# Seven-product MLP: products chained in PSUM banks, two weight pairs side by side in up, sums moved off GpSimd, down's operands in up's places

## The chip, the cores and the metric

The kernel runs on one NeuronCore of a Trainium2 chip. Times are device microseconds of one execution. A matmul runs on TensorE (PE in the rows, PEld for its weight loads); VectorE is DVE, ScalarE is ACT, GpSimd is POOL, SyncE is SP. DMA transfers are issued by the queues of SP and ACT here and are carried out by 16 DMA engines.

## The reference

One decoder layer of 1024 tokens of width 1024: a mixer (windowed attention, a gated short convolution and attention into memory tokens, one output projection) and then the part that the change is about, the MLP:

```
h2 = rms_norm(x, g_pre_mlp)
f = square(relu(h2 @ w_up))            # 1024x1024 @ 1024x4096
f = f @ w_down                         # 1024x4096 @ 4096x1024
x = x + rms_norm(f, g_post_mlp)
```

All of it is float32.

## The kernel before, in words

**Precision.** Every large product is computed from pairs of fp32r tiles: a "hi" part, a rounded copy written by ACT (`copy`, L88), and a "lo" part, the remainder, subtracted by DVE (`lo_part`, L92). Three matmuls (hi hi, hi lo, lo hi) make one product; `mm3` (L100 to L103) is the helper for it. So each operand tile costs one ACT and one DVE instruction before PE can use it; `split` does both.

**Seven products.** Up and down are computed by a Strassen/Winograd scheme: both matrices are cut into quarters, and 7 products of sums of quarters take the place of 8. For up, the hidden activations h2 (transposed, quarters b11, b12, b21, b22) are the fixed operand: the sums t1 to t4 are formed and split once. The weights come in 16 **pairs** (`p`) of two blocks of 128 columns; for each pair the sums s1 to s4 of the quarters a11, a12, a21, a22 are formed, and product `(p, i)` takes the weight form and the h2 form that `FORMS[i]` names. Each product is 12 matmuls of 128x512 into one PSUM bank; up has 16 x 7 x 12 = 1344 of them (L1107 to L1109).

**Up, per product.** `prep` (L1082) loads the pair's raw weights (`w_raw`, L1034, an SP transfer of 512 KB into one of 5 stage buffers), lets POOL form the four sums of the pair (`s_sums`, L1075 to L1079), and splits the product's weight form into a free slot `wop`. `product` (L1101) issues the matmuls, `product_out` (L1112) empties the bank: product 1 and product 2 share one bank, 5 and 3 share another, and every other product has its own. The four quarters of each result are put together by DVE additions in SBUF tiles `ef`, squared-relu is ACT (Relu, Square) or one DVE instruction (`relu2`, L1099), then the sums s1 to s4 of the activations (L1151 to L1154) are formed on DVE, and all of it is stored to DRAM by `f_out` (L1096) **on ACT's queue**. PE's order is written by hand: `seq` lists the products, pair after pair, each product's operand prepared by `prep_next` two places ahead in the program. For the first seven products the order of ACT, DVE and POOL is written by hand too (`manual_schedule`); after that a scheduler of the framework orders those engines and SP from the program's dependences.

**Head of up.** The last row tile of the out-projection (`y_mm`, `y_post_*`, `h2_turn`) is finished while PE already works on products 1 and 2 of pairs 0 to 2, which need only b11 and b21. t1 to t3 (`t_sums`, L1017) need the last row tile, t4 is one POOL instruction of 128x2048 (`raw_t4`, L1244).

**Down.** After up its pools are closed (`up_pool.close()`) and new ones opened. Down has 2 chunks (halves of the contraction), 7 products each in the order 1, 2, 7, 6, 5, 4, 3 and 1, 7, 6, 5, 4, 2, 3, and 4 steps to a product; a step is 24 matmuls of 128x512 into 4 banks (`sub_mm`, L1312), so 56 steps and 1344 matmuls. `prep2` (L1300) makes a step's operands, two steps ahead: one 128x1024 tile of stored activations (`fraw`, loaded by `a_load`) and one of w_down (`r_b`, loaded by `b_load`, or a DVE sum of two of them), each split, into one of 6 slots `op`. Each product has its own accumulator `acc` of 4 tiles (7 of them). `evict` (L1344) copies the banks out in chunk 0 (ACT) and adds in chunk 1 (DVE, L1352); POOL combines the seven accumulators while chunk 1 runs (L1355 to L1367). `piece` and `finish` do the last norm, the residual sum and the store of each row tile.

Of the kernel before, what the change touches and what calls it, by code (L numbers as in the profile page):

```python
# [45 lines left out]
def hybrid_block(ctx, tc, x, mem, positions, g_pre_mix, g_mem, w_in, w_mem_kv, conv_w, g_attn_out,  # L46
                 g_conv_out, g_xattn_out, w_out, g_post_mix, g_pre_mlp, w_up, w_down, g_post_mlp,
                 ident_in, bias_in, invf_in, out):
    nc = tc.nc
# [918 lines left out]
    for n in ("b11", "b21", "b22"):  # L968
        TM[n] = [p2.tile([128, 4, 512], R, name=n + s, tag=n + s) for s in "hl"]
    raw_pool = ExitStack()  # L970
    pr = raw_pool.enter_context(pool("h2raw", 1, side="right"))
    RB = {n: pr.tile([128, 4, 512], F, name="raw_" + n, tag="raw_" + n) for n in ("b11", "b22", "b12", "b21")}
    yb_pool = ExitStack()
    yb = yb_pool.enter_context(pool("yb", 2, side="right"))
# [17 lines left out]
    def y_post_add(st, r):  # L992
        xr, ob = XR[st], OB[st]
        for h in range(2):
            cl = slice(h * 512, (h + 1) * 512)
            v.scalar_tensor_tensor(xr[:, cl], ob[:, cl], r, xr[:, cl], op0=OP.mult, op1=OP.add)
        nc.sync.dma_start(x1_d[st * 128:(st + 1) * 128], xr)
        s2 = small.tile([128, 1], F, name="s1b", tag="s1b")
        sumsq(s2, xr, 1024)
        return s2  # L1000
# [16 lines left out]
    def t_sums(i):  # L1017

        cl = slice(i * 128, i * 128 + 128)
        b11, b12, b22 = (RB[n][:, :, cl] for n in ("b11", "b12", "b22"))  # L1020
        v.tensor_sub(b11, b12, b11)
        v.tensor_sub(b12, b22, b12)
        v.tensor_sub(b22, b22, b11)

    T_OF = {"t1": "b11", "t2": "b22", "t3": "b12", "t4": "t4"}

    def t_split(n, c0, c1):
        split(TM[n][0][:, :, c0:c1], TM[n][1][:, :, c0:c1], RB[T_OF[n]][:, :, c0:c1])

# [14 lines left out]

    NPAIR = FF // 256
# [6 lines left out]
    SM, WO_, PB, EF = {}, {}, {}, {}  # L1052
    banks = [mm_bank, mm_bank, s_bank, s_bank, pt_bank, pt_bank, ot_bank, tp_bank]
    bn = [0]

    def next_bank():
        bn[0] += 1
        return banks[(bn[0] - 1) % 8]()
# [5 lines left out]
    def e_tile():  # L1064
        slot = e_free.pop(0)
        t = slot[0].tile([128, 512], F, name="ef", tag=slot[1]) if isinstance(slot[1], str) else slot[0][:, slot[1]]
        return slot, t
# [5 lines left out]
    def s_sums(p):  # L1073
        s1, s2, s3, s4 = (ps_.tile([128, 4, 128], F, name=f"s{i}", tag=f"s{i}") for i in range(1, 5))
        a11, a12, a21, a22 = (a_block(p, n) for n in ("a11", "a12", "a21", "a22"))  # L1075
        g.tensor_add(s1, a21, a22)
        g.tensor_sub(s2, s1, a11)
        g.tensor_sub(s3, a11, a21)
        g.tensor_sub(s4, a12, s2)  # L1079
        SM[p] = {"s1": s1, "s2": s2, "s3": s3, "s4": s4}  # L1080

    def prep(p, i):  # L1082

        n = FORMS[i][0]
        for ff in ([2 * p] if n in ("a11", "a12") else [2 * p, 2 * p + 1]):
            if ff not in WR:
                w_raw(ff)
        if n[0] == "s" and p not in SM:
            s_sums(p)
        slot, w = w_op()  # L1090
        split(w[:, 0], w[:, 1], SM[p][n] if n[0] == "s" else a_block(p, n))
        WO_[p, i] = slot, w

    def f_out(p, n, t):
        c, r = p // 8, p % 8 * 128
        nc.scalar.dma_start(f_d[c][n][r:r + 128], t)  # L1096

    def relu2(t):
        v.scalar_tensor_tensor(t, t, 0.0, t, op0=OP.max, op1=OP.mult)  # L1099

    def product(p, i):  # L1101
        th, tl = TM[FORMS[i][1]]
        slot, w = WO_.pop((p, i))
        prev = {2: 1, 3: 5}.get(i)
        b = PB[p, i] = PB[p, prev] if prev else next_bank()
# [6 lines left out]
    def product_out(p, i):  # L1112
        b = PB[p, i]
        e = EF.setdefault(p, {})
        if i == 1:
            e["u"] = e_tile()
            copy(e["u"][1], b)
        elif i == 2:
            t = (None, stage(512, name="ef")) if p < 3 else e_tile()
            nc.scalar.activation(t[1], b, AF.Relu)  # L1120
            nc.scalar.activation(t[1], t[1], AF.Square)
            f_out(p, "a11", t[1])
            if p > 2:
# [326 lines left out]
```

## Time and profile before

| what | value |
|---|---|
| time, median of 3 runs | 1220.71 us (1218.74 to 1222.88) |
| profiled execution, its own time | 1217.59 us |
| its span in the trace | 1215.8 us |
| PE busy | 1140.7 us, 94%, 5776 matmuls |
| DVE, ACT, POOL busy | 820.9, 579.7, 249.6 us |
| first matmul of up, last matmul of up | 535.85 us, 874.07 us |
| first matmul of down, last matmul of down | 882.88 us, 1206.29 us |

The span is what the trace covers; the profiled execution's own time has 1.8 us around it, and the median of the runs is 3.1 us above that execution. Everything up to about 535 us is the mixer. "Busy" adds up instructions, so 94% on PE does not say that only 6% can be won, nor where: that has to be read by stage.

### The profile page before, as it was taken

What the parts mean: (1) busy time and instruction counts of PE and PEld (TensorE: products, weight loads), DVE (VectorE), ACT (ScalarE), POOL (GpSimd) and SP (SyncE); (2) the same over time, 40 slices, a digit from 0 to 9 for tenths busy, and PEclk for the clock granted to TensorE, in tenths of its full rate; (3) what the DMA queues carried; (4) which work ended last, traced back from release to release, by engine and by line L of the source; (5) the groups of instructions that cost most, each with busy time, mean ns of one, the idle gap of its engine ahead of it and who ended that gap; (6) DMA issues with size and microseconds to landing.
All of it is one profiled execution on the core that took longest, in us unless ns stands there. A gap on an engine that the chain in (4) does not pass through costs nothing.

```text
span 1215.8 us, 15988 instructions
## 1 busy us (share of the span) xinstructions
PE 1140.7 (94%) x5776; PEld 966.1 (79%) x5776; DVE 820.9 (68%) x1380; ACT 579.7 (48%) x1096; POOL 249.6 (21%) x222
## 2 busy tenths in 40 slices
PE   6989999999999999986899999999789999999896
PEld 5879999897878778875778888888668888888684
DVE  6977676777677357657976666666466644697885
ACT  5675666657574445545333333333144454433342
POOL 2370201102020211104532222221000000025631
PEclk9989999999999999997999999999989999999898
DMA  7340100100212543333444444432493247332234
GB/s 228 122 118 6 48 23 18 38 8 9 67 31 62 164 166 139 121 112 96 147 156 149 150 153 155 156 130 104 159 368 122 98 162 263 135 103 90 85 132 180
DMA packets 119663, 145.05 MB, mean 119 GB/s; under 512 B 8736, under 2 KB 72864, under 8 KB 119584
## 3 DMA queue, kind: packets, MB, share of 16 engines
q1 hardware_dynamic: 103456, 114.67, 29.5%
q10 hardware_dynamic: 16128, 29.37, 6.5%
q8 instruction: 45, 0.74, 0.3%
q14 instruction: 34, 0.28, 0.1%
HBM read 102.06 MB, written 41.94 MB: 118 GB/s over the span
## 4 chain that ended last, share of the span: by engine, by line
PE 75%; DVE 10%; ACT 5%; DMA 4%; issue 3%; POOL 1%; SPq 1%; ACTq 0%; DVEq 0%; POOLq 0%
PE mm L101 7%; PE mm L102 7%; PE mm L103 7%; PE sc L103 3%; PE sc L101 3%; PE sc L102 3%; PE pt L103 2%; PE pt L102 2%; PE pt L472 2%; PE pt L101 2%; PE sc L1109 2%; PE mm L1107 2%; PE sc L1107 2%; PE sc L1108 2%; PE pt L1107 2%
## 5 line engine op out<-in xcount | busy, mean ns | idle before, releaser
L92 DVE TENSOR_TENSOR op<-fraw,op 128x1024 fp32r<-128x1024 f32 x56 | 71.5, 1280 | 88.0 <-ACT op L88 87.9
L88 ACT ACTIVATE op<-fraw 128x1024 fp32r<-128x1024 f32 x56 | 59.0, 1058 | 141.4 <-PE tp L103 65.2
L212 POOL TENSOR_TENSOR wl<-wraw,wh 128x384 fp32r<-128x384 f32 (+1 forms) x62 | 56.3, 936 | 293.1 <-ACT wh L88 291.4
L101 PE MATMUL mm<-wh,hh 128*128 128x384 f32 x256 | 91.5, 357 | 0.9 <-ACT wh L88 0.9
L102 PE MATMUL mm<-wl,hh 128*128 128x384 f32 x256 | 87.6, 342 | 0.3 <-DVE wl L212 0.2
L103 PE MATMUL mm<-wh,hl 128*128 128x384 f32 x256 | 87.6, 342 | 0.0
L92 DVE TENSOR_TENSOR op<-r_b,op 128x1024 fp32r<-128x1024 f32 x56 | 73.7, 1316 | 9.2 <-ACT op L88 9.2
L92 DVE TENSOR_TENSOR wop<-s,wop 128x512 fp32r<-128x512 f32 x64 | 49.3, 776 | 35.1 <-ACT wop L88 34.5
L88 ACT ACTIVATE wop<-wuraw 128x512 fp32r<-128x512 f32 x45 | 28.5, 633 | 91.2 <-DVE ef L1153 38.0
L92 DVE TENSOR_TENSOR tl<-pt,th 128x512 fp32r<-128x512 f32 (+1 forms) x96 | 60.0, 643 | 17.3 <-ACT th L88 16.5
L130 POOL TENSOR_TENSOR rstd<-ms,half_neg 128x1 f32<-128x1 f32 (+2 forms) x43 | 29.7, 692 | 193.8 <-DVE ms L127 177.3
L88 ACT ACTIVATE op<-r_b 128x1024 fp32r<-128x1024 f32 x56 | 58.6, 1046 | 12.8 <-PE sc L103 8.7
L461 ACT ACTIVATE P<-P,m 128x896 f32<-128x896 f32 (+3 forms) x64 | 49.7, 776 | 30.3 <-DVE m L459 29.6
L88 ACT ACTIVATE wop<-s 128x512 fp32r<-128x512 f32 x64 | 39.8, 628 | 49.7 <-PE pt L1109 9.4
L88 ACT ACTIVATE th<-pt 128x512 fp32r<-128x512 f32 (+1 forms) x96 | 52.3, 560 | 20.0 <-PE pt L472 18.1
L1358 POOL TENSOR_TENSOR acc<-acc,acc 128x512 f32<-128x512 f32 x4 | 8.0, 2030 | 225.9 <-DVE acc L1352 225.9
L101 PE MATMUL mm<-op 128*128 128x512 f32 x112 | 44.7, 399 | 8.4 <-ACT op L88 8.4
L101 PE MATMUL mm<-hh,wh 128*128 128x512 f32 x128 | 52.0, 406 | 0.0
L103 PE MATMUL mm<-hh,wl 128*128 128x512 f32 x128 | 50.9, 397 | 0.0
L102 PE MATMUL mm<-hl,wh 128*128 128x512 f32 x128 | 50.6, 396 | 0.0
L101 PEld LDWEIGHTS mm<-wh,hh 128*128 128x128 f32 x256 | 48.9, 191 | 1.5 <-ACT wh L88 1.3
L102 PEld LDWEIGHTS mm<-wl,hh 128*128 128x128 f32 x256 | 48.8, 191 | 1.3 <-POOL wl L212 0.7
(532 smaller groups left out, 3609.3 us busy)
## 6 DMA issues: line engine op xcount, KB each, us to landing
f_s<-ef ACTq DMA_DIRECT2D x64, 256.0 KB, 2.1
r_b<-in_w_down SPq DMA_DIRECT2D x32, 512.0 KB, 6.0
fraw<-f_s SPq DMA_DIRECT2D x32, 512.0 KB, 3.7
wuraw<-in_w_up SPq DMA_DIRECT2D x30, 512.0 KB, 4.5
f_a<-ef ACTq DMA_DIRECT2D x48, 256.0 KB, 2.9
fraw<-f_a SPq DMA_DIRECT2D x24, 512.0 KB, 3.9
wraw<-in_w_in SPq DMA_DIRECT2D x60, 128.0 KB, 2.7
woraw<-in_w_out SPq DMA_DIRECT2D x8, 512.0 KB, 3.8
```

The source lines that it names most:

```text
L88: nc.scalar.activation(o, i, AF.Copy, scale=scale)
L92: nc.vector.tensor_sub(lo, src, hi.bitcast(F))
L101: nc.tensor.matmul(o, a_hi, b_hi, start=first, stop=False)
L102: nc.tensor.matmul(o, a_hi, b_lo, start=False, stop=False)
L103: nc.tensor.matmul(o, a_lo, b_hi, start=False, stop=last)
L130: nc.gpsimd.tensor_tensor(r, ms, half_neg.to_broadcast([128, n]), op=OP.pow)
L212: eng.tensor_sub(wt[1][:, :cols], rv[:, k], wt[0][:, :cols].bitcast(F))
L461: nc.scalar.activation(p[:, :nk], p[:, :nk], AF.Exp, scale=-1.0, bias=m, accum_out=den[:, 2 * i + h:2 * i + h + 1])
L472: nc.tensor.transpose(t[:, n * 128:(n + 1) * 128], P[i][:, col:col + 128], ident)
L1107: nc.tensor.matmul(b, w[:, 0, k], th[:, k], start=(k == 0 and not prev), stop=False, skip_group_check=True)
L1108: nc.tensor.matmul(b, w[:, 0, k], tl[:, k], start=False, stop=False, skip_group_check=True)
L1109: nc.tensor.matmul(b, w[:, 1, k], th[:, k], start=False, stop=(k == 3), skip_group_check=True)
```

## The change

In up, two pairs run side by side: `seq` takes a block of two pairs and gives each product for the one pair and then for the other, in the order 1, 2, 6, 5, 7, 3, 4. Products are **chained in PSUM**: 6, 7 and 4 go on accumulating in the bank of product 1 (after it was copied or read out), 3 in that of product 5; the partial results that were DVE sums in SBUF are now what stands in the bank. POOL does none of the sums any more: `w_sum` forms the weight sums on DVE, `t_sums` forms t4 there too, a quarter at a time. The squared relu is always ACT. The stores of the activations go from ACT's queue to SP's. Operands are prepared three products ahead, and the order of ACT, DVE and SP in all of up is now that of the program's text. In down, operands and w_down tiles take the places of up's tiles (t1 to t3, b11, b21, b22, t4) instead of pools of their own, so the first three steps are prepared while up's last products run; the products go in the order 1, 5, 6, 3, 7, 2, 4 in both chunks, chained in the same way in two groups of four banks; 4 accumulators take the place of 7; operands are prepared three steps ahead, and POOL's sums are gone. The number of matmuls is the same, 1344 and 1344.

```diff
     def t_sums(i):
...
+        v.tensor_sub(b21, b21, b22)
...
-    def s_sums(p):
-        s1, s2, s3, s4 = (ps_.tile([128, 4, 128], F, name=f"s{i}", tag=f"s{i}") for i in range(1, 5))
...
-        g.tensor_add(s1, a21, a22)
-        g.tensor_sub(s2, s1, a11)
-        g.tensor_sub(s3, a11, a21)
-        g.tensor_sub(s4, a12, s2)
...
+    def w_sum(p, i):
...
+            v.tensor_add(SX[p], a21, a22)
...
     def prep(p, i):
...
+        for n in {6: (1, 2), 5: (4,), 7: (3,)}.get(i, ()):
+            w_sum(p, n)
+        w_hi(p, i)
+        w_lo(p, i)
...
     def f_out(p, n, t):
         c, r = p // 8, p % 8 * 128
-        nc.scalar.dma_start(f_d[c][n][r:r + 128], t)
-
-    def relu2(t):
-        v.scalar_tensor_tensor(t, t, 0.0, t, op0=OP.max, op1=OP.mult)
+        nc.sync.dma_start(f_d[c][n][r:r + 128], t)
+
+    def relu2(t, src=None):
+        nc.scalar.activation(t, t if src is None else src, AF.Relu)
+        nc.scalar.activation(t, t, AF.Square)
+
+    CHAIN = {6: 1, 7: 1, 4: 1, 3: 5}
 
     def product(p, i):
...
-        prev = {2: 1, 3: 5}.get(i)
-        b = PB[p, i] = PB[p, prev] if prev else next_bank()
+        prev = CHAIN.get(i)
+        if prev:
+            b = PB[p, prev]
+        elif i == 1:
+            b = PB[p, i] = (s_bank if p // 2 % 2 else mm_bank)()
+        else:
+            b = PB[p, i] = (pt_bank if i == 2 else tp_bank if p % 2 else ot_bank)()
...
     def product_out(p, i):
-        b = PB[p, i]
+
+        b = PB[p, CHAIN.get(i, i)]
...
+        if i in (1, 6, 5):
+            e[i] = e_tile()
+            copy(e[i][1], b)
         elif i == 2:
+            t = e[1][1]
+            v.tensor_add(t, b, t)
+            later.append(lambda: (relu2(t), f_out(p, "a11", t)))
...
+    for b in range(NPAIR // 2):
+        seq += [(p, i) for i in (1, 2, 6, 5, 7, 3, 4) if b > 1 or i > 2 for p in (2 * b, 2 * b + 1)]
...
+    ORDER = (1, 5, 6, 3, 7, 2, 4)
...
+    o_free = [(pt_, n + s) for n in ("t2", "t1", "t3") for s in "hl"] + [(yt, None)] * 2
...
+            elif n in (last + 9, last + 11, last + 13):
+                prep2(*steps[(n - last - 9) // 2])
...
-    acc = {i: pa.tile([128, 4, 512], F, name=f"acc{i}", tag=f"acc{i}") for i in range(1, 8)}
...
+    C = {q: pa.tile([128, 4, 512], F, name=f"c{q}", tag=f"c{q}") for q in (11, 22, 12)}
...
     def evict(c, i, st):
...
+        if c == 0 and i in (1, 6, 5, 4):
+            copy(t, b)
+        else:
+            v.tensor_add(t, b, t)
...
-    steps = [(c, i, s) for c in range(NCH) for i in ((1, 2, 7, 6, 5, 4, 3) if c == 0 else (1, 7, 6, 5, 4, 2, 3))
-             for s in range(NSUB)]
...
+    ahead_ = 3
```

**Head of up, DVE.** The lines below are DVE's order where products 1 and 2 give way to products that need t1 to t4 (`wop` a weight form, `ef` an accumulator of a result, `raw_b` the sums t in float32, `sx`, `sy` and `s` weight sums). Before:

```order
L92 TENSOR_TENSOR t2l<-raw_b_5367,t2h 128x4x128
L92 TENSOR_TENSOR wop<-wuraw,wop 128x512
L92 TENSOR_TENSOR t3l<-raw_b_5368,t3h 128x2048
L92 TENSOR_TENSOR wop<-s_6511,wop 128x512
L92 TENSOR_TENSOR t1l<-raw_b_5366,t1h 128x2048
L92 TENSOR_TENSOR wop<-yb,wop 128x512
L1126 TENSOR_TENSOR ef<-sc,ef 128x512
L92 TENSOR_TENSOR wop<-s_6512,wop 128x512
L92 TENSOR_TENSOR wop<-s_6510,wop 128x512
L92 TENSOR_TENSOR t4l<-raw_t_6354,t4h 128x2048
```

And in the changed kernel:

```order
L92 TENSOR_TENSOR wop<-wuraw,wop 128x512 x2
L92 TENSOR_TENSOR t2l<-raw_b_5374,t2h 128x4x128
L1081 TENSOR_TENSOR sx<-wuraw 128x512
L1084 TENSOR_TENSOR sy<-sx,yb 128x512
L1081 TENSOR_TENSOR sx<-wuraw 128x512
L1084 TENSOR_TENSOR sy<-sx,yb 128x512
L92 TENSOR_TENSOR wop<-sy,wop 128x512 x2
L1147 TENSOR_TENSOR ef<-pt,ef 128x512
L1088 TENSOR_TENSOR sy<-yb,sy 128x512
L92 TENSOR_TENSOR t1l<-raw_b_5373,t1h 128x2048
```

Four weight sums that were POOL's stand in DVE's queue ahead of the operands of products (0,6) and (1,6), and the large t1, t3 and t4 parts come after those.

**Between up and down, ACT.** The lines below are ACT's order from the end of up into down (`f_s` and `f_a` are the stored activations in DRAM, `op` the operands of down). Before:

```order
L1096 DMA f_a_1_5409<-ef 128x512
L1096 DMA f_a_1_5407<-ef 128x512
L1096 DMA f_s_1_5410<-ef 128x512
L1096 DMA f_s_1_5412<-ef 128x512
L1096 DMA f_s_1_5411<-ef 128x512
L1096 DMA f_s_1_5408<-ef 128x512
L88 ACTIVATE op<-fraw 128x1024
L88 ACTIVATE op<-r_b_8834 128x1024
L88 ACTIVATE op<-fraw 128x1024
```

And in the changed kernel:

```order
L88 ACTIVATE wop<-wuraw 128x512
L1116 ACTIVATE ef<-ef 128x512
L1117 ACTIVATE ef<-ef 128x512
L88 ACTIVATE op<-fraw 128x1024
L88 ACTIVATE op<-r_b_8552 128x1024
L88 ACTIVATE wop<-wuraw 128x512
L88 ACTIVATE op<-fraw 128x1024
L1116 ACTIVATE ef<-ef 128x512
```

The first operands of down (`op<-fraw`) stood behind all six stores of the last pair; now the stores are gone from this queue, and two of them stand ahead of the last weight form (`wop<-wuraw`) of up.

## Rows read from the trace of the kernel before

**Rows 1.** The page: busy time, share of the span and instructions of each engine.
```profile
PE 1140.7 (94%) x5776; PEld 966.1 (79%) x5776; DVE 820.9 (68%) x1380; ACT 579.7 (48%) x1096; POOL 249.6 (21%) x222
```
**Rows 2.** Busy time by stage: from:to, length, PE, PEld, DVE, ACT, POOL, PEclk, DMA share, GB/s.
```profile
535.00:628.00 93.00, 75.56 (x295) 58.68 (x294) 74.66 (x83) 38.62 (x61) 40.15 (x23) 0.89 0.41 130
628.00:874.00 246.00, 246.00 (x1065) 199.61 (x1064) 150.14 (x219) 87.08 (x146) 56.96 (x44) 1.00 0.41 136
...
951.00:1125.00 174.00, 174.00 (x769) 144.09 (x768) 111.90 (x95) 75.18 (x84) 24.81 (x14) 1.00 0.42 144
1125.00:1181.00 56.00, 51.61 (x219) 42.22 (x218) 47.65 (x56) 23.72 (x37) 26.19 (x16) 0.94 0.29 101
```
**Rows 3.** PE's waits from 510 to 1216 us: us in total, times, longest.
```profile
PE mm L101 <- ACT op L88: 8.4, 1, 8.4
PE pt L102 <- DVE op L92: 4.4, 1, 4.4
PE pt L101 <- ACT op L88: 3.9, 2, 2.6
```
**Rows 4.** PE's timeline over up: start, us, engine, line, op, tiles, idle before.
```profile
535.85 0.48 PE L1107 MATMUL mm<-b11h,wop 128*128 128x512 f32 x1
...
545.83 0.63 PE L1108 MATMUL mm<-b21l,wop 128*128 128x512 f32 x1
546.26 0.63 PE L1109 MATMUL mm<-b21h,wop 128*128 128x512 f32 x1
...
627.18 0.51 PE L1107 MATMUL tp<-b21h,wop 128*128 128x512 f32 x1 [1.36 <-ACT ef L88]
...
874.07 0.39 PE L1109 MATMUL ot<-b22h,wop 128*128 128x512 f32 x1
```
**Rows 5.** PE's timeline over down.
```profile
882.88 0.80 PE L101 MATMUL mm<-op 128*128 128x512 f32 x1 [8.42 <-ACT op L88]
...
929.70 0.39 PE L101 MATMUL pt<-op 128*128 128x512 f32 x1
...
1125.54 0.39 PE L101 MATMUL mm<-op 128*128 128x512 f32 x1
...
1181.31 0.39 PE L101 MATMUL pt<-op 128*128 128x512 f32 x1
```
**Rows 6.** DVE by line and shape, 540 to 628 us: busy us, mean ns, idle before.
```profile
L92 DVE TENSOR_TENSOR wop<-s,wop 128x512 fp32r<-128x512 f32 x17 | 16.8, 1008 | 0.8 <-ACT wop L88 0.6
...
L92 DVE TENSOR_TENSOR t2l<-raw_b,t2h 128x512 fp32r<-128x512 f32 x1 | 4.5, 4520 | 0.7 <-ACT t2h L88 0.7
```
**Rows 7.** The same on DVE, 628 to 874 us.
```profile
L92 DVE TENSOR_TENSOR wop<-s,wop 128x512 fp32r<-128x512 f32 x48 | 33.2, 692 | 34.3 <-ACT wop L88 33.9
L92 DVE TENSOR_TENSOR wop<-wuraw,wop 128x512 fp32r<-128x512 f32 x35 | 30.2, 862 | 0.7 <-ACT wop L88 0.7
```
**Rows 8.** The same on ACT, 628 to 874 us.
```profile
L88 ACT ACTIVATE wop<-s 128x512 fp32r<-128x512 f32 x47 | 29.6, 629 | 31.8 <-PE sc L1109 9.0 <-PE mm L1109 7.4 <-PE pt L1109 7.2
```
**Rows 9.** The page's DMA issues: KB each, median us from issue to landing.
```profile
wuraw<-in_w_up SPq DMA_DIRECT2D x30, 512.0 KB, 4.5
```
**Rows 10.** ACT's timeline between up and down.
```profile
876.72 4.05 ACTq L1096 DMA_DIRECT2D f_s<-ef  x4
880.82 1.06 ACT L88 ACTIVATE op<-fraw 128x1024 fp32r<-128x1024 f32 x1 [9.85 <-DMA f_s<-ef]
```
**Rows 11.** DVE by line and shape, 951 to 1125 us.
```profile
L92 DVE TENSOR_TENSOR op<-r_b,op 128x1024 fp32r<-128x1024 f32 x32 | 43.3, 1354 | 0.0
L92 DVE TENSOR_TENSOR op<-fraw,op 128x1024 fp32r<-128x1024 f32 x32 | 40.9, 1278 | 61.1 <-ACT op L88 61.1
L1303 DVE TENSOR_TENSOR r_b<-r_b,r_b 128x1024 f32<-128x1024 f32 x19 | 24.4, 1290 | 0.8 <-DMA r_b<-in_w_down 0.5
L1352 DVE TENSOR_TENSOR acc<-pt,acc 128x512 f32<-128x512 f32 x4 | 2.6, 682 | 0.0
```
**Rows 12.** The same on ACT, 951 to 1125 us.
```profile
L88 ACT ACTIVATE op<-fraw 128x1024 fp32r<-128x1024 f32 x32 | 33.9, 1061 | 90.2 <-PE tp L103 46.5 <-PE sc L103 43.6
```
**Rows 13.** DVE's timeline in chunk 1 of down, beside POOL's sums of accumulators.
```profile
1136.39 1.78 DVE L1360 TENSOR_TENSOR acc<-acc,acc 128x512 f32<-128x512 f32 x1
```

More of the change, by code (lines that the diff above doesn't have):

```diff
@@ L1159, in hybrid_block @@
+            later.append(last)
+        return later
     end = NS - 1
@@ L1254, in hybrid_block @@
-    raw_pool.close()
-    with tc.manual_schedule(engines={PE}):
+        prep(2, 2)
+        prep(3, 2)
+        load_next()
+        load_next()
+        load_next()
+        t_hi("t2", 384, 512)
+        t_lo("t2", 384, 512)
+        product_out(2, 1)
+        product(3, 1)
+        for p in (0, 1):
+            w_sum(p, 1)
+            w_sum(p, 2)
+        w_hi(0, 6)
+        product_out(3, 1)
+        product(2, 2)
+        w_hi(1, 6)
+        w_lo(0, 6)
+        w_lo(1, 6)
+        late = product_out(2, 2)
@@ L1310, in prep2 @@
+            split(hi, lo, raw)
+            res.append((slot, hi, lo))
         OPS[c, i, s] = res
+        if i == 2:
+            v.tensor_sub(RT["b12", s], RT["b21", s], RT["b11", s])
+    todo = seq[3:]
+    last = len(seq) - 14
+    late = []
+    with tc.manual_schedule(engines={PE, ACT, DVE, SP}):
+        for n, x in enumerate(seq):
+            if n == 3:
+                t_hi("t4")
+                t_lo("t4")
+                e4 = pr4.tile([128, 4, 512], F, name="ef", tag="raw_b21")
+            if todo:
+                y = todo.pop(0)
+                prep(*y)
+                if y[1] in (7, 4):
+                    if y[0] < 2 and y[1] == 7:
+                        w_free.append((yb, "yb"))
+                    else:
+                        load_next()
+            for f in late:
+                f()
+            product(*x)
+            if n == last + 2:
+                for s in range(NSUB):
+                    b_load(0, "b11", s)
+            elif n == last + 5:
+                for s in range(NSUB):
+                    b_load(0, "b12", s)
+            elif n in (last + 9, last + 11, last + 13):
+                prep2(*steps[(n - last - 9) // 2])
+            if n == last + 12:
+                for s in range(NSUB):
+                    b_load(0, "b22", s)
+            late = product_out(*x)
+            if n == 3:
+                e_free += [(e4, i) for i in range(4)]
+        WD["b21"] = (pt4, "t4")
+        for f in late:
+            f()
+        for s in range(NSUB):
+            b_load(0, "b21", s)
@@ new lines, in hybrid_block @@
+    NEXT = {7: ("b22",), 2: ("b11", "b21"), 4: ("b12",)}
+    ahead_ = 3
+    with tc.manual_schedule(engines={PE, SP}):
+        while len(a_todo) > len(steps) - 8:
+            a_load()
+        for n, (c, i, s) in enumerate(steps):
+            m = n + ahead_
+            if m < len(steps):
+                prep2(*steps[m])
+                c2, i2, s2_ = steps[m]
+                if c2 + 1 < NCH:
+                    for q in NEXT.get(i2, ()):
+                        b_load(c2 + 1, q, s2_)
+                if a_todo:
+                    a_load()
+            if (c, i, s) == (1, 1, 0):
+                for t, (pl, tag) in enumerate(((yb, "yb"), (yb, "yb"), (gx, "g_pm"), (gx, "g_po"))):
+                    x_load(t, pl.tile, tag=tag)
+            if (c, i) == (NCH - 1, 4) and s:
```

403 lines of the change are left out of this document (187 added, 216 removed).

## The prediction

> **What bounds the kernel now.** I read the page's busy shares first [rows 1]: PE is busy 94% of the span, so at first sight there is little to win. Both kernels issue 1344 matmuls in up and 1344 in down, so the change can only win what PE loses to waits and to a low clock, and the question is how much of that lies in the MLP. The table by stage answers [rows 2]: from 628 to 874 us and from 951 to 1125 us PE is busy all the time at a clock of 1.00; from 535 to 628 it is busy 75.56 of 93 us at a mean clock of 0.89, from 1125 to 1181 51.61 of 56 at 0.94. So the MLP has two clean stretches and three leaking ones: the head of up, the passage from up to down with down's first steps, and the middle of chunk 1.
>
> The clean stretches give PE's own pitch. In up, 89 products of 12 matmuls start at 627.18 and the last matmul at 874.07 [rows 4]: (874.07 + 0.23 - 627.18) / 1068 = 0.2314 us a matmul, 2.777 a product. In down, 36 steps of 24 matmuls lie between 929.70 and 1125.54 [rows 5]: 5.44 us a step, 0.2267 a matmul.
>
> What is lost is the difference:
> - Up: from 535.85 to 874.30 are 338.45 us [rows 4]. 1344 matmuls at 0.2314 are 311.0, the last row tile's transposes, at the same pitch for eight or so, some 0.8. Lost: 26.6 us.
> - Passage: 874.30 to 882.88 [rows 4, 5]: 8.6 us, nearly all in one wait for ACT [rows 3].
> - Down until its last product at 1181.31: 298.43 us [rows 5] for 52 steps, 282.9 at the clean pitch. Lost: 15.5 us, among them the waits of 4.4 and 3.9 [rows 3].
>
> Together 50.7 us. Part of it is clock: after the longer waits about 12 matmuls start 0.43 us apart instead of 0.23 (545.83 to 546.26 [rows 4]), the lower of the two levels; that is 12 x 0.2 = 2.4 us on top of such a wait. The rest of the span, 34.5 us from 1181.31 to 1215.8, is the last product and the last norms.
>
> **The change part by part.** *Head of up.* Before, t2's last quarter took 4.52 us on DVE for 128x512 and the weight forms 1008 ns a piece [rows 6], against 692 in the clean stretch [rows 7]: POOL worked beside them. Those POOL sums are gone. In exchange DVE has them in its own queue. From the start of the last row tile's h2 work (537.25 us on DVE) to the lo part of product (0,6) the changed order holds some 32 instructions of 128x512 at 0.69 [rows 7] (5 for the last tile's turns and norm and t2's last quarter, 8 for t_sums, 7 weight forms, 2 accumulators, 4 weight sums, and xr, the norm and three quarters of t2, which count as 6), with the waits for two square roots 24.3 us, and with its waits for ACT about 26: ready at about 563. PE has eight products by then, 22.2 us, and the turn: through at about 559. So PE waits 4 to 4.5 us once or in two pieces, and with one spell of the low clock I put 7 us, within 0 (DVE runs in step) and 10 (two spells).
>
> *Steady up.* Per pair PE needs 7 x 2.777 = 19.4 us. DVE has 7 lo parts (4 at 0.692, 3 at 0.862 [rows 7]: 5.4), 4 weight sums, 3 additions from PSUM and 4 sums of results at 0.69 (7.6): 13.0 us. ACT has 7 hi parts, 3 copies and 8 instructions for four squared relus, 18 at 0.60 to 0.63 [rows 8]: 11.2 us. Both stay under 19.4 and operands are three products, 8.3 us, ahead. Before, DVE was busy 150.14 and ACT 87.08 of 246 us there [rows 2] and PE did not wait; it has 61% before and 67% now. I cost this part at nothing; PE's matmuls cover it, and if that cover went (DVE above 19.4 us a pair), every us more would be a us. Up's pitch itself could change with the places of the tiles; between down's 0.2267 and as much above 0.2314 that is -6 to +6 us. I take 0, since the same tiles are read in the same way for the most part.
>
> *Stores on SP.* The stores leave ACT's queue, on which four of them took 4.05 us while down's first operand stood behind them [rows 10]. On SP they stand ahead of loads. A store waits there for its result, and the next load behind it with it. The trace has a weight load at 4.5 us from issue to landing [rows 9]; the changed order issues loads six products, 16.7 us, ahead of their first use. So a store may hold the queue 12 us before PE is late, and a pair's results come within that. Nothing, then. The Trainium skill (Perfetto Trace Analysis, DMA Optimizations) advises the opposite of this edit: one issuing engine for inputs, another for outputs. No run here shows yet what it costs on this chip; by that rule there would be a loss, which is a rival below.
>
> *Passage.* ACT's 9.85 us of idle time before the first operand of down [rows 10] came from the stores and from pools that close behind up. Now three steps are prepared among up's last products, so most of the 8.6 us go. What remains: step 3's operands take places of up's last weight forms, and DVE's part for the fourth slot waits for PE's last product but one, with step 2's parts behind it. I put 1.5 us, within 0 and 6 (a wait of 3.5 and one low spell).
>
> *Down.* A step costs ACT 2 x 1.06 [rows 12] and DVE two lo parts of 1.28 [rows 11], four products in seven a subtraction of 1.29 a step, each product 4 additions of 0.68. A product of DVE is thus 13.0 or 18.1 us against PE's 21.8. In chunk 1 come the norm's products and the last sums of four row tiles, at 0.7 each: about 138 us over the 152 of the seven products, one product (2) above 21.8 by some 6. Operands are three steps, 16.3 us, ahead, where they were two; POOL's sums, beside which a DVE addition took 1.78 [rows 13] instead of 0.68 [rows 11], are gone. So I take off the whole 15.5 us and add nothing; what may come is the first rival.
>
> *Tail.* The order inside the last product is as it was, and its last operand has to wait for slots as before: a wait of about 2.8 us where it was 2.6 [rows 3]. No change.
>
> **Sum.** 1215.8 - 50.7 + 7 + 1.5 = 1173.6 us of span. With the 1.8 around it the profiled execution comes to 1175.4, against 1217.59; the median of the runs stood 3.1 above the profiled execution, so 1178.5 against 1220.71.
>
> **The rivals.** *Part of the waits stays.* DVE's order is a queue: one instruction that waits for a slot holds what stands behind it. For it: chunk 1 loads DVE to 138 of 152 us, and there the norms of finished tiles stand between operands. Against it: the lead of 16.3 us. Price: four waits of the kind seen [rows 3], 2.6 us and a low spell of 2.4 each, 20 us: 1198.
>
> *Chained banks wait.* Each of the 64 chained products in up (6, 7, 4 and 3 of 16 pairs) may start only when its bank has been read. Before, only two of seven products were chained (2 on 1, 3 on 5). If PE had to stand through a copy or an addition, 0.60 to 0.69 us and the handing over about as much, it would pay 1.3 us each, 83 us: 1262, slower. It decides where the reading lags more than three products behind, since between a product and the next on its bank lie three others, 8.3 us; ACT and DVE have 11.2 and 13.0 us of work per 19.4, so their lag should stay under two products. The Trainium skill (Perfetto Trace Analysis, Matmuls) says that independent groups should rotate through different banks so that the emptying of one overlaps the next; chaining gives up that rotation, and side by side with the second pair it gets part of it back. I give it 2%.
>
> *SP's queue.* If stores hold the loads of a block back for longer than those 12 us, PE waits in each of the six blocks that still load; 7 us a block, which the trace cannot exclude, would eat the 42 us won: 1220, no change, and more would be slower. For it: before, the loads stood on SP alone. Against it: the stores are waited for in the order in which they become ready. 3%.
>
> *It doesn't do what it says.* If the scheduler had moved the operands of down behind the last stores again, the passage would stay, 8 us: 1186. The order shows them ahead, so this is small and within the first rival's range.
>
> **How the numbers follow.** The forecast has 76%, the first rival, from 1186 to 1198 and a little beyond, 19%, SP's queue 3%, the chained banks 2%. The low end has head and passage without a new wait, 1170, and some of the pitch's 6 us: 1167. The high end is the first rival's 1198. A measurement of this kernel can tell about 0.3%, 3.7 us, from no change; faster than that are the forecast and nearly all of the first rival: 95%. Within 0.3% half of SP's queue, 2%; slower the other half and the chained banks, 3%.
>
> **What would show it.** In the changed profile PE's waits between 535 and 565 us should come to some 4 us for DVE's or ACT's weight forms of (0,6); from there to the last product of up PE should be busy throughout, DVE at about 67% and ACT at 58% of it; the gap between up and down should be under 3 us; in down no wait above 2 us before the last product, and POOL nearly idle. Wrong would be the forecast if PE waits for a bank (a wait of a product for ACT's copy or DVE's addition of the same tile), if a weight load lands after its first reader is due, if PE's pitch in up leaves 0.2314, or if DVE has no idle time in chunk 1.

## Result and profile after

| | before | changed |
|---|---|---|
| time, median of 4 runs each | 1219.72 us | 1171.69 us (1170.72 to 1174.99) |
| ratio of the times | | 0.9607, 95% interval 0.958 to 0.9635 |
| span of the profiled execution | 1215.8 us | 1169.3 us |
| forecast | | 1178.5 us, range 1167 to 1198 |

The change makes the kernel 48 us faster. Two runs of later experiments are left out, one of e5 at a mean granted clock of 0.557 (1868 us) and one of m1 at 0.849 (1254 us); the first is the one with the profile, so e5 has times and no trace that can be read.

The page of the changed kernel, its busy shares, against [rows 1]:

```profile
PE 1124.3 (96%) x5776; PEld 958.1 (82%) x5776; DVE 785.9 (67%) x1396; ACT 622.7 (53%) x1180; POOL 101.2 (9%) x129
```

PE has the same 5776 matmuls and is busy 96% instead of 94%: read by share alone, this would look like two per cent. The table by stage of the changed kernel, against [rows 2] (from:to, length, PE, PEld, DVE, ACT, POOL, PEclk, DMA share, GB/s):

```profile
536.00:558.00 22.00, 19.57 (x90) 15.05 (x88) 17.07 (x27) 14.07 (x26) 1.39 (x2) 1.00 0.32 99
558.00:851.00 293.00, 293.00 (x1270) 238.29 (x1271) 188.11 (x284) 164.59 (x276) 0.00 (x0) 1.00 0.53 171
...
996.00:1134.00 138.00, 138.00 (x610) 114.31 (x609) 94.77 (x97) 58.62 (x73) 0.00 (x0) 1.00 0.29 100
1134.00:1169.00 35.00, 23.86 (x97) 18.92 (x95) 23.19 (x48) 6.41 (x16) 6.37 (x8) 0.86 0.50 180
```

Of the three leaking stretches only the head has waits left, some 2 us; from 558 to 1134 us PE is busy without a break at a clock of 1.00, through the passage too. All that PE waits for from 510 us on (us in total, times, longest), against [rows 3]:

```profile
PE mm L1421 <- DVE op L92: 2.5, 1, 2.5
PE sc L1134 <- DVE wop L92: 1.2, 1, 1.2
PE pt L1134 <- DVE wop L92: 0.9, 1, 0.9
PE ot L1013 <- DVE ob L138: 0.2, 1, 0.2
```

And the marks of PE's timeline, which answer to [rows 4, 5] (start, us, ..., idle before):

```profile
536.69 0.48 PE L1132 MATMUL mm<-b11h,wop 128*128 128x512 f32 x1
...
557.96 0.50 PE L1134 MATMUL pt<-b21h,wop 128*128 128x512 f32 x1 [0.94 <-DVE wop L92]
...
851.09 2.92 PE L1421 MATMUL pt<-op 128*128 128x512 f32 x12
...
1134.01 2.88 PE L1421 MATMUL mm<-op 128*128 128x512 f32 x12
...
1145.02 7.14 PE L1421 MATMUL mm<-op 128*128 128x512 f32 x23 [2.46 <-DVE op L92]
```

With the pitches of the prediction the accounts are:

| part | before: lost | changed | difference |
|---|---|---|---|
| start of up | 535.85 | 536.69 | +0.8 |
| up | 26.6 | 851.09 - 536.69 - 311.0 - 0.8 = 2.6 | -24.0 |
| passage | 8.6 | 0 | -8.6 |
| down to its last product | 15.5 | 1134.01 - 851.09 - 282.9 = 0.0 | -15.5 |
| last product and norms | 34.5 | 1169.3 - 1134.01 = 35.3 | +0.8 |

The sum is -46.5, the difference of the spans. In the kernel before, PE's timeline puts 8.7 of down's 15.5 us, waits and low clock together, into its first five steps (3.3, 2.7 and 2.7 in those from 882.88, 902.45 and 910.63 us) and 6.8 into the step from 1141.86 us, in chunk 1.

### The profile page after: what moved, and what is told of

The parts are those of the page before. It is cut to its first block, busy times and chain, and to the rows that moved or that the text cites. A ratio compares the mean times of both kernels' runs of the same rounds, so it can differ in the third digit from the quotient of the medians.

```text
span 1169.3 us, 15898 instructions
## 1 busy us (share of the span) xinstructions
PE 1124.3 (96%) x5776; PEld 958.1 (82%) x5776; DVE 785.9 (67%) x1396; ACT 622.7 (53%) x1180; POOL 101.2 (9%) x129
## 4 chain that ended last, share of the span: by engine, by line
PE 83%; DVE 7%; ACT 3%; DMA 3%; issue 2%; POOL 1%; SPq 1%; DVEq 0%; POOLq 0%; ACTq 0%
PE pt L1421 6%; PE mm L1421 6%; PE sc L1421 6%; PE mm L101 6%; PE mm L103 6%; PE mm L102 6%; PE tp L1421 3%; PE ot L1421 3%; PE sc L1132 2%; PE sc L1134 2%; PE mm L1132 2%; PE sc L1133 2%; PE mm L1134 2%; PE mm L1133 2%; PE pt L472 2%; PE sc L407 2%
## 5 line engine op out<-in xcount | busy, mean ns | idle before, releaser
L92 DVE TENSOR_TENSOR op<-fraw,op 128x1024 fp32r<-128x1024 f32 x56 | 68.5, 1223 | 92.4 <-ACT op L88 92.4
L1421 PE MATMUL mm<-op 128*128 128x512 f32 x336 | 82.3, 395 | 2.5 <-DVE op L92 2.5
L1421 PE MATMUL pt<-op 128*128 128x512 f32 x336 | 80.7, 389 | 0.0
L1421 PE MATMUL sc<-op 128*128 128x512 f32 x336 | 80.4, 389 | 0.0
L1421 PEld LDWEIGHTS mm<-op 128*128 128x128 f32 x336 | 64.2, 191 | 16.4 <-DVE op L92 2.9
L1421 PEld LDWEIGHTS pt<-op 128*128 128x128 f32 x336 | 63.1, 188 | 13.1
L1421 PEld LDWEIGHTS sc<-op 128*128 128x128 f32 x336 | 63.1, 188 | 13.1
L92 DVE TENSOR_TENSOR op<-r_b,op 128x1024 fp32r<-128x1024 f32 x56 | 68.2, 1218 | 0.8 <-ACT op L88 0.8
L1116 ACT ACTIVATE ef<-ef 128x512 f32<-128x512 f32 x48 | 30.3, 631 | 63.5 <-DVE ef L1155 34.3
L102 PE MATMUL mm<-hl,wh 128*128 128x512 f32 x128 | 50.7, 396 | 0.0
```

The source lines that it names most:

```text
L92: nc.vector.tensor_sub(lo, src, hi.bitcast(F))
L102: nc.tensor.matmul(o, a_hi, b_lo, start=False, stop=False)
L1116: nc.scalar.activation(t, t if src is None else src, AF.Relu)
L1421: nc.tensor.matmul(b, x[:, k, cl], y[:, k], start=(first and s == 0 and k == 0 and m == 0), stop=(s == NSUB - 1 and k == 1 and m == 2), sk ...
```

## Experiments: undoing one part of the change

The theory: PE gained nothing from the chaining itself; the time came from waits that go with GpSimd beside DVE, with the order of ACT's and DVE's queues, and with how early operands are ready. Rivals: the stores' queue, the lead in down, the work taken off DVE, the distance between products on one bank. The kernels of this section are the changed kernel with one edit. None of them takes out the chaining alone, so the theory's first clause rests on the waits in the traces and on b4.

**e1, stores on ACT's queue again.**

```diff
-        nc.sync.dma_start(f_d[c][n][r:r + 128], t)
+        nc.scalar.dma_start(f_d[c][n][r:r + 128], t)
```

> The changed kernel with one edit: the stores of the activations go back to ACT's queue. A pair has 7 stores of about 1 us each on that queue (four took 4.05 us in the kernel before), so ACT has 11.2 + 7 = 18 of the 19.4 us that PE needs for a pair. Theory (the queue matters, since the stores stand ahead of weight forms and of down's first operands): PE waits in up and at the passage, 3 to 15 us together, 1175 to 1187 us. Rival (the queue is indifferent, the gain came from GpSimd and from the lead of the operands): 1170 to 1174, no new wait of PE. Rival from the notes on separate issuing engines for inputs and outputs: faster than the changed kernel, under 1169.

1199.36 us, ratio to before 0.9821 (0.9797 to 0.9845): more than half of the gain is lost, more than any theory said. Up takes 328.4 instead of 314.4 us, down until the last product's wait 306.4 instead of 293.9. ACT's timeline in up shows the mechanism:

```profile
699.98 2.40 ACTq L1113 DMA_DIRECT2D f_s<-ef  x3
702.43 0.63 ACT L1116 ACTIVATE ef<-ef 128x512 f32<-128x512 f32 x1 [3.81 <-DVE ef L1155]
...
703.63 0.62 ACT L88 ACTIVATE wop<-wuraw 128x512 fp32r<-128x512 f32 x1
705.61 1.66 ACTq L1113 DMA_DIRECT2D f_s<-ef  x3
707.31 0.60 ACT L1116 ACTIVATE ef<-sc 128x512 f32<-128x512 f32 x1 [3.06 <-PE mm L1134]
```

Single stores of this queue issue in 0.33 us, so it is not the issue time that I had priced at 1 us. A store of a sum waits in ACT's queue until DVE has made the sum, and the next weight form waits behind it: ACT idles 3.8 and 3.1 us here though PE is about to need it. What PE pays in up is small each time, at a clock of 1.00: it waits for weight forms, mostly of product 2, block after block (PE's waits from 510 us on), and loses some 1.5 us a block of two pairs.

```profile
PE pt L1132 <- ACT wop L88: 3.1, 6, 0.7
```

At the passage the same: the stores of the last pairs stand between the operands of down, and PE waits 4.6 us for ACT in down's first product. So in this hand-written order the store belongs on an engine that computes nothing.

**e2, the weights' sums on GpSimd again.**

```diff
-            v.tensor_add(SX[p], a21, a22)
+            g.tensor_add(SX[p], a21, a22)
...
-            v.tensor_sub(SY[p], a12, SY[p])
+            g.tensor_sub(SY[p], a12, SY[p])
```

> The changed kernel with the sums of the weights back on GpSimd, t4 still on DVE. Theory (GpSimd beside DVE costs in the head alone, where DVE's queue is what PE waits for; elsewhere DVE's idle third takes it): in the head lo parts go from 0.69 to about 1.0 us and the first two pairs' sums take 1.4 to 1.8 us each, one after the other, so (0,6) is 3 to 6 us later and a spell of the low clock comes with it: 1174 to 1181; from 570 us to the end of up PE still has no wait, DVE's weight forms 0.75 to 1.0 us. Rival (GpSimd beside DVE was all of what up lost): most of the 24 us come back, 1185 to 1196, with waits all through up. Rival (the sums' engine is indifferent): 1170 to 1173.

1174.56 us, 0.9624 (0.9606 to 0.9643). (POOL's order is that of the program's text here too.) Up takes 3.0 us more (317.4). In up PE's waits lie in the head alone; the first row is the last product of down, as in the changed kernel:

```profile
PE mm L1421 <- DVE op L92: 2.4, 1, 2.4
PE sc L1134 <- DVE wop L92: 2.3, 1, 2.3
PE ot L1013 <- DVE ob L138: 1.3, 1, 1.3
```

From 575 us on lo parts of sums run slower than the 692 ns they take in the changed kernel, and PE does not notice (DVE by line and shape, busy us, mean ns, idle before):

```profile
L92 DVE TENSOR_TENSOR wop<-sy,wop 128x512 fp32r<-128x512 f32 x30 | 23.9, 800 | 34.7 <-ACT wop L88 34.7
```

The theory's case. The time alone would not tell it from no change, since the two intervals overlap; the waits do.

**e3, two steps of lead in down.**

```diff
-    ahead_ = 3
+    ahead_ = 2
...
-            elif n in (last + 9, last + 11, last + 13):
+            elif n in (last + 9, last + 11):
```

> The changed kernel with down's operands prepared two steps ahead, as before, where it has three. Theory (down lost its 15.5 us to GpSimd's sums of accumulators beside DVE and to its order, and two steps, 10.9 us, are enough without them): 1171 to 1175, with perhaps one wait of 1 to 3 us at the passage or in chunk 1. Rival (the third step of lead is what takes the waits away): waits at product boundaries in chunk 1 and at the passage, 8 to 15 us, 1180 to 1187.

1172.34 us, 0.9605 (0.9585 to 0.9625): no difference, and no new wait of PE. The third step of lead buys nothing here.

**e4, pairs one after the other from pair 4 on.**

```diff
+            seq += [(p, i) for p in (2 * b, 2 * b + 1) for i in (1, 2, 6, 5, 7, 3, 4)]
...
-        loads += [4 * b, 4 * b + 2, 4 * b + 1, 4 * b + 3]
+        loads += [4 * b, 4 * b + 1, 4 * b + 2, 4 * b + 3]
```

> The changed kernel with the pairs from 4 on one after the other, so that only one product (2.8 us) instead of three (8.3 us) lies between a product and the next one on its bank. Theory (a chained product pays only for what is left of the reading of its bank when PE comes to it; the copy or addition takes 0.6 to 0.7 us and is asked for in time): few waits under 1 us each, 1171 to 1182. Rival (chaining costs a wait per chained product unless other products cover it): 48 chained products at 1 to 1.5 us and some low clock, 1215 to 1245.

1185.45 us, 0.971 (0.9688 to 0.9733), 14 us more; but not for the reason that either side gave. From pair 4 to the last, with one product between two on a bank, PE waits once for a bank, 0.60 us at 625.63. Then, at the end of up, it waits 6.5 us for a weight form. SP's queue there (queue, line, transfer; the first row is its wait in total, times, longest):

```profile
SPq L1338 <- PE sc L1134: 13.5, 1, 13.5
```
```profile
822.84 0.32 SPq L1113 DMA_DIRECT2D f_a<-ef  x1
836.72 1.92 SPq L1338 DMA_DIRECT2D r_b<-in_w_down  x4
...
839.25 0.41 SPq L1113 DMA_DIRECT2D f_a<-ef  x1
839.75 2.70 SPq L1338 DMA_DIRECT2D r_b<-in_w_down  x4
844.05 4.32 SPq L1113 DMA_DIRECT2D f_s<-ef  x3
```

and DVE behind it:

```profile
847.34 0.69 DVE L1163 TENSOR_TENSOR ef<-ef 128x512 f32<-128x512 f32 x1 [11.43 <-DMA f_a<-ef]
```

A load of w_down takes the place of b11 and must wait for PE's last product with b11, which in this order comes later. SP stands still for 13.5 us, a store behind the load is late, DVE may not overwrite the stored tile for 11.4 us, and the weight form behind that on DVE is what PE misses. So SP's queue can cost PE time, though not on the path that the rival named: there stores were to hold back weight loads, here a load held back a store. It reached PE as 6.5 us and a spell of the low clock. In the changed kernel SP waits up to 12.6 us at a time in up, for a place for a weight load, and PE does not wait. That side by side the two pairs reach their last use of b11 early enough is read from this, not tried by itself.

**e5, down's first operands prepared only after up.**

```diff
-            elif n in (last + 9, last + 11, last + 13):
-                prep2(*steps[(n - last - 9) // 2])
...
+        for x in steps[:3]:
+            prep2(*x)
```

> The changed kernel with the operands of down's first three steps prepared only behind up's last product, not among its last five. Theory (the passage is won by preparing early, not by the stores leaving ACT's queue, since moving those alone left the kernel before at its time): a gap of 4 to 7 us before down's first matmul and a further wait of 1 to 3 in its first two products, with the low clock 6 to 12 us: 1178 to 1184. Rival (the places taken over by last use, with no pool closed between, are what matters): a gap under 2 us, 1171 to 1174.

Three runs from 1178.74 to 1181.03 us, ratio 0.9673 (0.9658 to 0.9688): 8 us more than the changed kernel, within the theory's range; its gap and waits can't be read. But 8 us is less than half of what the kernel before lost at this place, 8.6 at the passage and 8.7 in down's first five steps. So late operands give back 8 of these 17.3 us, and 9 stay won with late operands. Whether those 9 come from the places taken over by last use, from loads issued earlier or from something else, no run shows.

## Experiments: one part alone in the kernel before

**b1, weight sums and t4 on DVE.**

```diff
-        g.tensor_add(s1, a21, a22)
+        v.tensor_add(s1, a21, a22)
...
-        g.tensor_sub(RB["t4"], RB["b22"], RB["b21"])
+        v.tensor_sub(RB["t4"], RB["b22"], RB["b21"])
```

> The kernel before with one edit: the weights' sums and t4 go from GpSimd to DVE, all else as it was (its own order, two banks chained of seven, pairs one after the other). Theory (GpSimd beside DVE is the largest part of what the head of up lost): t2's last quarter falls from 4.52 to 0.7 us, the weight forms of the head from 1.0 to 0.7; DVE's queue gets 8 sums of 0.69 and 2.3 us for t4 instead; PE's waits between 540 and 628 us fall from 19 us by 6 to 12, 1208 to 1214. Rival (the sums merely change queues, DVE is what PE waits for): within 1217 to 1224. Steady up shows no wait in either.

1212.21 us, 0.9931 (0.9909 to 0.9952). Up takes 330.4 instead of 338.45 us, 8.0 less; the weight forms of sums in the head take 682 ns where they took 1008 [rows 6]. PE's waits in up fall from 17.4 to 11.8 us, a little less than the theory's 6 to 12. Two waits of the head stay as they were, and they are not DVE's (PE's timeline of this kernel):

```profile
546.81 0.80 PE L1107 MATMUL mm<-b21h,wop 128*128 128x512 f32 x1 [3.54 <-ACT ef L88]
...
562.20 0.74 PE L1107 MATMUL sc<-b21h,wop 128*128 128x512 f32 x1 [3.49 <-ACT ef L88]
```

**b2, stores on SP's queue.**

```diff
-        nc.scalar.dma_start(f_d[c][n][r:r + 128], t)
+        nc.sync.dma_start(f_d[c][n][r:r + 128], t)
```

> The kernel before with one edit: the stores of the activations go from ACT's queue to SP's. Theory (in the kernel before the stores cost PE something at the passage alone, since up had no wait from 628 to 874 us with them on ACT): the gap before down's first matmul falls from 8.6 us by 3 to 5, 1214 to 1218. Rival (stores on ACT cost the kernel before as much as they cost the changed kernel when put back there, 28 us): 1190 to 1200. Rival (on SP they hold back down's loads): 1220 to 1228.

1219.46 us, 0.9997 (0.9985 to 1.0008): nothing. The gap at the passage does fall, as the theory said, from 8.6 to 4.4 us, and then comes back in down's first two products (PE's waits from 870 to 960 us):

```profile
PE pt L101 <- ACT op L88: 4.7, 1, 4.7
PE mm L101 <- ACT op L88: 4.2, 1, 4.2
PE mm L102 <- DVE op L92: 1.6, 1, 1.6
```

The wait for ACT was 2.6 there and is 4.7 now, that for DVE 0.7 and 1.6: the operands are late anyway, PE meets them at another place. From the last matmul of up to the matmul behind the wait in chunk 1 it takes 271.6 us, where it took 272.3.

**b3, accumulators' sums on DVE.**

```diff
-            g.tensor_add(A_[6], A_[6], A_[1])
+            v.tensor_add(A_[6], A_[6], A_[1])
...
-            g.tensor_add(A_[3], A_[3], a)
+            v.tensor_add(A_[3], A_[3], a)
```

> The kernel before with one edit: the sums of the seven accumulators in chunk 1 of down go from GpSimd to DVE. Theory (beside GpSimd DVE took 1.78 us for an addition of 0.68): the waits of 4.4 and 0.7 us near 1142 fall to 0 to 2, with the low clock 4 to 7 us less, 1213 to 1217. Rival (24 more additions of 0.69 on DVE, 17 us in 60, put its queue behind PE): waits of 3 to 10 us more, 1222 to 1232.

1213.55 us, 0.9943 (0.9923 to 0.9964). The wait of 4.4 us in chunk 1 is gone (one of 1.3 us for DVE stands at 1123.20 instead), and DVE's additions of this line take 0.682 us where one took 1.78 [rows 13]:

```profile
L1360 DVE TENSOR_TENSOR acc<-acc,acc 128x512 f32<-128x512 f32 x4 | 2.7, 682 | 0.0
```

DVE took on 24 additions of about 0.7 us and was still nearly in time: what it lost beside GpSimd was more.

**b4, all three.**

> The kernel before with the three edits together and nothing of the chaining, of the side-by-side pairs or of the places and the lead in down. Theory (chaining and side by side give PE nothing by themselves, where the engines have room; the queues do): the sum of the three, 1203 to 1211, what is left to the changed kernel is the head's order and the passage. Rival (without chaining, which takes 6 of 10 DVE instructions from a pair, DVE cannot carry the sums): 1216 or more.

1205.84 us, 0.9887 (0.9865 to 0.9909): 14 us, the sum of the three (7.8, 0.5 and 6.4). So the sums off GpSimd, with the stores moved and no other part of the change, are worth 14 of the 48 us, and without chaining DVE can carry them. In its profiled execution (span 1198.6, the shortest of five by 5 us) up takes 327.6 us, 13 more than in the changed kernel, and the passage with the first products still waits 4.3, 1.6 and 4.7 us.

## Where up's remaining loss was, and a version faster than both

After b4 the question was what the 13 us more in up are. PE's timeline of the kernel before has part of the answer in rows that I had counted only in the sum:

```profile
545.24 0.79 PE L1107 MATMUL mm<-b21h,wop 128*128 128x512 f32 x1 [3.54 <-ACT ef L88]
...
560.65 0.75 PE L1107 MATMUL sc<-b21h,wop 128*128 128x512 f32 x1 [3.50 <-ACT ef L88]
...
603.54 0.47 PE L1107 MATMUL mm<-b22h,wop 128*128 128x512 f32 x1 [3.40 <-DVE ef L1133]
603.84 0.39 PE L1108 MATMUL mm<-b22l,wop 128*128 128x512 f32 x1
604.07 0.39 PE L1109 MATMUL mm<-b22h,wop 128*128 128x512 f32 x1
...
627.18 0.51 PE L1107 MATMUL tp<-b21h,wop 128*128 128x512 f32 x1 [1.36 <-ACT ef L88]
```

All four are chained products: product 2 on the bank of product 1, product 3 on that of 5, waiting until the bank has been copied or added. They are 11.8 of the 17.4 us that PE waits in up. The first two bring a spell of the low clock each (2.4 us); behind the third the matmuls start 0.23 us apart, so there the clock stayed up, as it did behind the fourth. That makes some 16.6 of the 26.6. The third and the fourth belong to GpSimd's share as well: both are gone in b1, and are 4.8 of its 8 us. The first and the second stay in b1, and in b4 as 3.5 and 1.9 us.

Of b4's 13 us these two are thus only a part. As much is waits for the weight form of the first product that needs t2, (0,6) (PE's timeline of b4):

```profile
563.47 0.50 PE L1107 MATMUL sc<-t2h,wop 128*128 128x512 f32 x1 [3.05 <-ACT wop L88]
...
566.81 0.79 PE L1109 MATMUL sc<-t2h,wop 128*128 128x512 f32 x1 [2.61 <-DVE wop L92]
```

PE comes to (0,6) after six products there, and after eight in the changed kernel (at 563.19 us), where products 1 and 2 of four pairs stand ahead of it instead of three. On b4's DVE the sum t4 (2.28 us from 563.87) and the sums of the weights stand ahead of its lo part (566.07). No kernel here changes this order alone, so how the 13 us divide between the order, the pairs side by side and the chaining is not shown.

The first of the four waits stood behind one instruction on ACT (ACT's timeline of the kernel before):

```profile
543.55 1.06 ACT L135 ACTIVATE sq<-xr 128x1024 bf16<-128x1024 f32 x1 [4.52 <-issue]
...
544.61 0.58 ACT L88 ACTIVATE ef<-mm 128x512 f32<-128x512 f32 x1
```

The copy of product (0,1) stands behind the norm's square, which waits 4.5 us. In the changed kernel the copy is at 540.29 us, ahead of that square, and product 2 has a bank of its own, so there is nothing to wait for:

```profile
540.29 0.59 ACT L88 ACTIVATE ef<-mm 128x512 f32<-128x512 f32 x1
542.86 1.06 ACT L135 ACTIVATE sq<-xr 128x1024 bf16<-128x1024 f32 x1 [1.98 <-issue]
```

That the order decides and not the distance fits e4, where one product between two on a bank cost 0.6 us once in 12 pairs; a kernel that moves the copy alone was not run.

Two losses are left in the changed kernel that its trace names. First, up's pitch. Of the products after the eighth whose rows stand alone, 48 have weight form and h2 operand in the same half of SBUF (below or above 128 KB of a partition) and ran at a mean of 0.2278 us a matmul; 55 have them in different halves and ran at 0.2332. Second, the last product: the lo parts of the last step stand on DVE behind norms of finished tiles (DVE's timeline of the changed kernel):

```profile
1140.71 1.22 DVE L92 TENSOR_TENSOR op<-fraw,op 128x1024 fp32r<-128x1024 f32 x1
1142.35 1.41 DVE L1443 SCALAR_TENSOR_TENSOR x1r<-c,rstd,x1r 128x512 f32<-128x512 f32 x2 [0.43 <-POOL rstd L130]
...
1143.75 1.22 DVE L92 TENSOR_TENSOR op<-r_b,op 128x1024 fp32r<-128x1024 f32 x1
```

Three kernels try them.

**m1, weight forms in the operand's half.**

```diff
+        slot = (w_free[side] or w_free[1 - side]).pop(0)
...
+        WO_[p, i] = w_op(FORMS[i][1][0] == "b" or FORMS[i][1] == "t4")
...
+        pw2 = e4_pool.enter_context(pool("wops2", 1, side="right"))
+        w_free[1] += [(pw2, f"wop{i}") for i in range(2)]
-        pe2 = e4_pool.enter_context(pool("efs2", 1, side="right"))
-        e_free += [(pe2, f"ef{i}") for i in range(4)]
```

> The changed kernel with the weight forms of up put into that half of SBUF (below or above 128 KB of a partition) in which the product's h2 operand lies; two of its slots lie elsewhere and there are 12 result tiles instead of 16. In the changed kernel's trace 48 products with both in the same half ran at a mean of 0.2278 us a matmul, 55 with them in different halves at 0.2332; 56 of the 64 latter ones change. Theory (PE's pitch depends on the halves): 56 x 12 x 0.0054 = 3.6 us less, 1167 to 1169, all products from the ninth on at 0.2265 to 0.230, no new wait of PE. Rival (the pitch goes with the tile itself, not with the halves): 1170 to 1173, 0.2332 for b22 and t4 as before. Rival (the 12 result tiles are too few): waits of ACT or DVE for stores reach PE, 1175 or more.

1167.72 us, 0.9574 (0.9561 to 0.9587), 4 us less than the changed kernel. The waits of the head stand as before, and from the second of them to up's last matmul the same 1270 matmuls take 288.66 us, 0.2273 each; in the changed kernel it was 293.13, 0.2308. The products with b22 and t4, nearly all at 0.233 in the changed kernel, run at 0.2267 to 0.2288, so the pitch does not go with the tile itself. PE's timeline of m1, from that matmul to down's first:

```profile
558.05 0.50 PE L1134 MATMUL pt<-b21h,wop 128*128 128x512 f32 x1 [0.96 <-DVE wop L92]
...
846.71 2.91 PE L1421 MATMUL pt<-op 128*128 128x512 f32 x12
```

**m2, the norms of row tiles 0 to 3 behind the last operands.**

```diff
                 piece(st, 0, t)
-                finish(st, (t, C[12][:, st]))
...
                 if s == NSUB - 1:
+                    for st in range(4):
+                        finish(st, (C[11][:, st], C[12][:, st]))
```

> The changed kernel with the last norms of row tiles 0 to 3 put behind the operands of down's last step in the program's order. Theory (the wait of 2.5 us in the last product is DVE's queue: the lo parts of the last step stand behind those norms, 1140.7 and 1143.7 us, though their hi parts are done at 1135.3 and 1136.9): the wait and its 1.8 us of low clock go, 3 to 4.5 us less, 1167 to 1169. Rival (the norms then end later and the end stays where it is, since the chain of the last four row tiles at 4.5 us each is longer than PE's 4.1): 1170 to 1172.

1168.92 us, 0.9581 (0.9567 to 0.9594). PE's wait of 2.5 us and its low clock are gone; PE ends 4.4 us earlier counted from down's start, the kernel 2.9 us earlier counted from up's start, since the last norms on DVE, 4.53 us a row tile, now set the end. Both the theory and its rival are partly right.

**m3, both, and the gain's product in a tile of its own.**

```diff
-        v.tensor_mul(src, src, g_po2[:, h * 512:(h + 1) * 512])
+        v.tensor_mul(src if dst is None else dst, src, g_po2[:, h * 512:(h + 1) * 512])
...
-                piece(4 + st, 0, t)
-                finish(4 + st, (t, C[22][:, st]))
+                d = RT["b22", st][:, 0]
+                piece(4 + st, 0, t, d)
+                finish(4 + st, (d, C[22][:, st]))
```

> The changed kernel with both edits, and with the product by the gain in the last four row tiles written to a free tile, so that it need not wait until ACT has read the sum. Theory: 3.6 + 3.5 us and some 0.8 us from the last chain, 1163 to 1165. Rivals as for the two alone; if the last chain decides, 1166 to 1168.

1163.48 us, 0.954 (0.9527 to 0.9553): the fastest here, 8 us below the changed kernel and 56 below the one before. In place, the product by the gain waited 0.85 us for ACT's read of the same tile (DVE's timeline of the changed kernel):

```profile
1158.65 0.69 DVE L1435 TENSOR_TENSOR c<-c,gain 128x512 f32<-128x512 f32 x1 [0.85 <-ACT sq L135]
```

Now it runs beside that read, and a row tile of the last four takes 3.93 us (1150.50 to 1154.43 in DVE's timeline of m3) instead of 4.53:

```profile
1150.50 0.68 DVE L1454 TENSOR_TENSOR c<-sc,c 128x512 f32<-128x512 f32 x1
1151.21 0.69 DVE L1435 TENSOR_TENSOR r_b<-c,gain 128x512 f32<-128x512 f32 x1
...
1153.10 0.75 DVE L1443 SCALAR_TENSOR_TENSOR x1r<-r_b,rstd,x1r 128x512 f32<-128x512 f32 x1 [0.72 <-POOL rstd L130]
...
1154.43 0.68 DVE L1454 TENSOR_TENSOR c<-sc,c 128x512 f32<-128x512 f32 x1
```

## Why the prediction was right, and where it was not

- *What is lost in the MLP* held: 50.7 us against a clean pitch, of which the changed kernel gave back 48.1 (24.0, 8.6 and 15.5). The method, two clean stretches as a measure for the leaking ones, carried the forecast.
- *Head of up*, 7 us, was mis-sized: it is 2.6. DVE took 24.3 us from 538.09 us, where its last-tile work begins, to the lo part of (0,6), done at 562.4, and not 26: the instructions were 21.4 us instead of 22.1, the waits for the square roots 1.2 instead of 2.2, those for ACT 1.5 instead of 1.7. And I forgot that PE itself is delayed ahead of (0,6), by two weight forms among other things (1.2 and 0.9 us), so that it arrives at 563 and waits there for nothing. In pieces of at most 1.3 us the waits brought no low clock: the table by stage has 1.00 from 536 to 558.
- *Why the head leaked* was told wrongly. I put it on GpSimd beside DVE; b1 shows that as 8 us of 24. Chained products that wait for late copies and additions, which the text priced only as a danger of the change, were 11.8 us of waits, 4.8 of them within b1's share. What is left of up's gain after b4, 13 us, is argued from waits and not shown by an edit. The sum did not suffer, since it took the loss as a whole.
- *Stores on SP, nothing*: right, but by luck of the two orders. In the kernel before the stores' queue was indifferent (b2); in the changed kernel it is worth 28 us (e1). The rule that I weighed there (the Trainium skill, Perfetto Trace Analysis, DMA Optimizations: one issuing engine for inputs and another for outputs) says only that this may make sense; with ACT as the second engine it makes this kernel slower, and the measurement decides.
- *Passage*, 1.5 us, is 0; e5 shows 8 of the 17 us lost there and in down's first steps as the price of late operands. *Down*, 0, is 0.0; DVE's load in chunk 1 was put too high, 138 of 152 us where it is 104.0 of 152.4, and with it the chance of the first rival. *Steady up*, 0, is 0, with DVE busy 64% and ACT 56% (188.11 and 164.59 of 293).
- *Tail*, no change, is +0.8, but its rows were misread: the wait of 2.6 us that it names lies in down's first products, at 910.63 us. The last product of the kernel before has waits of 1.3, 0.5 and 0.6 us at a clock of 1.00 (the 1.3 is counted in the 3.9 that the prediction puts ahead of it); the changed kernel has one of 2.46 us and a spell of the low clock behind it.
- The rest of the difference, 2.5 of the 6.8 us between 1178.5 and 1171.69, is the step from the profiled execution to the median: 3.1 us before, 0.6 now.
- The rivals: chained banks cost the changed kernel no wait and e4 one of 0.6 us, and were a cost of the kernel before; SP's queue cost nothing here and about 14 us in e4, by another path; part of the waits stays did not come.

Left open: what part of the 28 us of e1 each store has, since only all of them were moved; how up's 13 us beyond b4 and the 9 us at the passage that e5 does not give back came about; and why the halves of SBUF matter to PE, and where the border between them lies.

## To carry to other kernels

Measure PE's pitch in a clean stretch and subtract; what a change of order can win is that difference, not the idle share. In an in-order queue ask of each instruction that waits (a store, a norm's square, a load into a place still read) who stands behind it: here that question found 28 us (e1), some 17 (the chained products of the kernel before) and 14 (e4), where the work itself fitted easily. And a chained bank cost nearly nothing here, 0.6 us in e4, as long as the engine that reads it was not held by something else.

## What was not expected of the hardware

PE's pitch depends on where the two operands of a matmul lie in SBUF: 0.2273 us a matmul where both are in the same half for nearly all products, 0.2308 where half of the products cross, with PE's waits as they were (m1, 4 us of 1172). By product it was 0.2278 and 0.2332 in the changed kernel. The tiles were compared as they happened to lie, below or above 128 KB; whether the border is there was not tried.
